# Rotating a 268 MB matrix by 90 degrees: borrowing the output buffers for the first two loads, dividing the last macro tile, and halving the last store

## The chip, the cores and the metric

The kernel runs on one core of one Trainium2 chip. Times are device microseconds of one execution. Groups of experiments ran on different chips, each beside its own runs of before, and only ratios are compared between groups. Ratios are computed as the mean time of one kernel's fast runs over the mean time of the other's fast runs of the same rounds on the same chip, so they are not quite the ratio of the medians that are quoted beside them. Kernels are counted "faster" or "slower" only beyond 2%.

## The reference

```python
def setup_inputs():
    return {"x": np.random.randn(8192, 8192).astype(np.float32), "k": 1}

def reference(x, k):
    return np.rot90(x, k)        # out[8191 - c, r] = x[r, c]
```

There is no arithmetic: 268 MB are read, 268 MB are written, and in between every element changes its place.

## The kernel before

The matrix is worked off in macro tiles of 1024 rows and 4096 columns. Each macro tile takes eight loads of 128 rows by 4096 columns (2 MB), which VectorE (DVE) copies into 64 small chunks, reversing the order of the columns within each block of 128. Then eight output groups follow: TensorE transposes 32 blocks of 128 by 128 into PSUM, ScalarE (ACT) evicts them in two copies, and one store writes 2 MB.

```python
R = 1024; RT = R // P; CH = 512; G = 4; PW = 2          # P = 128
def widths(first, last, M):
    return [M // 2] * 2
...
a_pool = ctx.enter_context(tc.tile_pool(name="a_pool", bufs=2))    # load buffers, 16 KB a partition
r_pool = ctx.enter_context(tc.tile_pool(name="r_pool", bufs=68))   # chunks, 2 KB a partition
o_pool = ctx.enter_context(tc.tile_pool(name="o_pool", bufs=2))    # output buffers, 16 KB a partition
psum_pool = ...                                                    # bufs=2, 8 KB a partition each
for r0 in range(0, N, R):
    c0 = 0
    for C in widths(r0 == 0, r0 + R == N, M):
        for t in range(RT):
            a = a_pool.tile([P, C], dt, tag="a")
            nc.sync.dma_start(out=a[:], in_=x[r0 + t*P : r0 + (t+1)*P, c0 : c0 + C])
            for j in range(C // CH):
                ... nc.vector.tensor_copy(...)     # each block's columns reversed, into a chunk
        for g0 in range(0, C // P, G):
            o = o_pool.tile([P, G, R], dt, tag="o")
            for h in range(0, G, PW):
                ... nc.tensor.transpose(...)       # 16 times into ps
                nc.scalar.copy(o[:, G - PW - h : G - h, :], ps[:])
            ...
            nc.scalar.dma_start(out=dst, in_=o[:]) # dst: four runs of 4 KB a partition
        c0 += C
```

A function `whole_reads`, run over the finished program, matters later. A store reads its 16 KB a partition from a contiguous output buffer, but the program describes that as four pieces of 1024 elements; `whole_reads` rewrites the source as one piece of 4096. The loads read one run of 16 KB a partition from the start.

Of the kernel before, what the change touches and what calls it, by code (L numbers as in the profile page):

```python
# [2 lines left out]

# [5 lines left out]

P = 128  # L10




R = 1024
RT = R // P
CH = 512
G = 4
PW = 2


def whole_reads(nc):






    for fn in nc.m.functions:
        for block in fn.blocks:  # L30
            for n, ins in enumerate(block.instructions):
                if not isinstance(ins, mybir.InstDMACopy):
                    continue
                src = ins.ins[0]
                ap = [list(d) for d in src.ap]
                if len(ap) == 3 and ap[2][0] == 1 and ap[1][0] == ap[2][1]:
                    ap = [ap[0], [1, 1], [1, ap[1][1] * ap[2][1]]]
                    block.instructions[n] = copy.replace(
                        ins,
                        ins=[copy.replace(src, ap=ap)],  # L40
                        ant_dge_precooked=False,
                    )


def widths(first, last, M):

    return [M // 2] * 2


@with_exitstack  # L50
def kernel(
    ctx: ExitStack,
    tc: tile.TileContext,
    x: bass.AP,
    k: bass.AP,
    out: bass.AP,
):
    nc = tc.nc
    assert k == 1, f"only k=1 supported, got {k}"
    nc.at_finalize(whole_reads)  # L60

    N, M = x.shape
    dt = x.dtype

    consts = ctx.enter_context(tc.tile_pool(name="consts", bufs=1))
    ident = consts.tile([P, P], dt)
    make_identity(nc, ident)

    a_pool = ctx.enter_context(tc.tile_pool(name="a_pool", bufs=2))
    r_pool = ctx.enter_context(tc.tile_pool(name="r_pool", bufs=68))  # L70
    o_pool = ctx.enter_context(tc.tile_pool(name="o_pool", bufs=2))
    psum_pool = ctx.enter_context(
        tc.tile_pool(name="psum", bufs=2, space=bass.MemoryType.PSUM)
    )

    for r0 in range(0, N, R):
        c0 = 0
        for C in widths(r0 == 0, r0 + R == N, M):
            chunks = {}
            for t in range(RT):  # L80
                a = a_pool.tile([P, C], dt, tag="a")
                nc.sync.dma_start(  # L82
                    out=a[:], in_=x[r0 + t * P : r0 + (t + 1) * P, c0 : c0 + C]
                )


                for j in range(C // CH):
                    ar = r_pool.tile([P, CH // P, P], dt, tag="ar")
                    nc.vector.tensor_copy(  # L89
                        out=ar[:],  # L90
                        in_=a[:, j * CH : (j + 1) * CH].rearrange(
                            "r (b m) -> r b m", m=P
                        )[:, :, ::-1],
                    )
                    chunks[t, j] = ar

            for g0 in range(0, C // P, G):
                o = o_pool.tile([P, G, R], dt, tag="o")
                for h in range(0, G, PW):
                    ps = psum_pool.tile([P, PW, R], mybir.dt.float32)  # L100
                    for w in range(PW):
                        g = g0 + h + w
                        for t in range(RT):
                            nc.tensor.transpose(  # L104
                                ps[:, PW - 1 - w, t * P : (t + 1) * P],
                                chunks[t, g * P // CH][:, g % (CH // P), :],
                                ident,
                            )
                    nc.scalar.copy(o[:, G - PW - h : G - h, :], ps[:])  # L109

                top = M - c0 - (g0 + G) * P
                dst = out[top : top + G * P, r0 : r0 + R].rearrange(
                    "(g m) f -> m g f", g=G
                )
                nc.scalar.dma_start(out=dst, in_=o[:])  # L115
            c0 += C


# [1 line left out]
_INS = ['x', 'k']  # L120
_OUTS = [((8192, 8192), 'float32')]

_NUMBERS = {'k': 1}


# [26 lines left out]
```

## Time and profile before

The median was 1278.4 us in three runs (1276.62 to 1279.38). The profiled execution took 1282.29 us, so it is a little slower than those runs.

First the page of the profile of before: busy time of PE, the busy tenths of the DMA engines and the rate in 40 equal slices, the two DMA queues (packets, MB, share of the engines' time; q1 carries the loads, q10 the stores), and the DMA issues (size, median us from issue to landing).

```profile
span 1280.5 us, 10385 instructions
...
PE 720.3 (56%) x4096; PEld 686.7 (54%) x4096; DVE 355.2 (28%) x1024; ACT 467.0 (36%) x257; POOL 0.7 (0%) x6
...
DMA  9999999999999999999999999999999999999988
GB/s 346 364 421 425 426 426 424 429 429 428 429 430 427 430 425 431 425 431 427 426 428 429 430 422 426 428 428 426 429 429 424 425 426 426 428 426 427 427 352 357
...
q1 hardware_dynamic: 18432, 268.44, 49.9%
q10 hardware_dynamic: 18432, 268.44, 49.4%
...
a<-in_x_dram SPq DMA_DIRECT2D x128, 2048.0 KB, 16.6
out_dram<-o ACTq DMA_DIRECT2D x128, 2048.0 KB, 15.9
```

The DMA engines are busy 90% or more in all but the last two slices. They move 421 to 431 GB/s from the third slice to the 38th, less in the first two (346 and 364) and in the last two (352 and 357), and TensorE is busy 56%. The kernel is a DMA stream with a slow start and a slow end. Both queues sent 18432 packets for 128 transfers (the page counts 4096 packets under 512 B, 16 for each of the 256 transfers). Where this text says packet, it means this record of the profile.

The head, in the timeline of before (start, duration, engine, line, operation, count, idle time before it and its releaser):

```profile
8.18 2.77 DVE L89 COPY ar<-a 128x512 f32<-128x512 f32 x8 [8.18 <-DMA a<-in_x_dram]
...
13.05 2.77 DVE L89 COPY ar<-a 128x512 f32<-128x512 f32 x8 [2.09 <-DMA a<-in_x_dram]
...
19.81 2.78 DVE L89 COPY ar<-a 128x512 f32<-128x512 f32 x8 [3.99 <-DMA a<-in_x_dram]
...
25.66 2.77 DVE L89 COPY ar<-a 128x512 f32<-128x512 f32 x8 [3.07 <-DMA a<-in_x_dram]
...
50.54 2.77 DVE L89 COPY ar<-a 128x512 f32<-128x512 f32 x8 [2.65 <-DMA a<-in_x_dram]
...
57.06 0.66 ACTq L115 DMA_DIRECT2D out_dram<-o  x1
```

DVE starts on a load when it has landed: all its 871.5 us of waits end with a load (below). The first two loads were queued together and landed 4.87 us apart. Later ones come 5.4 to 6.9 us apart, because there are only two load buffers and each next load is issued after the 2.8 us of copies that free one. The eighth load landed at 50.5 us, and the first store was issued at 57.06.

The waits of before (engine, line, what it waited for: total us, times, longest):

```profile
DVE ar L89 <- DMA a<-in_x_dram: 871.5, 128, 9.3
ACT o L109 <- DMA out_dram<-o: 750.7, 125, 11.5
```

DVE waits for loads and ACT waits for stores all along: both sides wait for the DMA.

The tail, in stretches of before (from:to, length, busy us and number of instructions of PE, weight loads, DVE, ACT, POOL; granted clock, DMA share, GB/s):

```profile
600.00:680.00 80.00, 47.93 (x263) 45.80 (x261) 22.20 (x64) 29.10 (x16) 0.00 (x0) 0.72 1.01 428
...
1220.00:1240.00 20.00, 15.25 (x110) 14.25 (x108) 2.77 (x8) 11.02 (x6) 0.00 (x0) 0.82 0.81 340
1240.00:1260.00 20.00, 13.27 (x100) 12.48 (x101) 0.00 (x0) 13.24 (x8) 0.00 (x0) 0.91 0.87 369
1260.00:1281.00 21.00, 7.05 (x63) 6.50 (x61) 0.00 (x0) 8.57 (x5) 0.00 (x0) 0.77 0.80 338
```

The last load's copies and the last two evictions of before, in its timeline:

```profile
1223.92 2.77 DVE L89 COPY ar<-a 128x512 f32<-128x512 f32 x8 [7.02 <-DMA a<-in_x_dram]
...
1269.37 3.63 ACT L109 COPY o<-ps 128x2048 f32<-128x2048 f32 x2 [2.50 <-DMA out_dram<-o]
```

The middle runs at 428 GB/s. The last load's copies start at 1223.92 us, nine stores are issued after that, and while stores run alone the rate is 338 to 369 GB/s.

### The profile page before, as it was taken

What the parts mean: (1) busy time and instruction counts of PE and PEld (TensorE: products, weight loads), DVE (VectorE), ACT (ScalarE), POOL (GpSimd) and SP (SyncE); (2) the same over time, 40 slices, a digit from 0 to 9 for tenths busy, and PEclk for the clock granted to TensorE, in tenths of its full rate; (3) what the DMA queues carried; (4) which work ended last, traced back from release to release, by engine and by line L of the source; (5) the groups of instructions that cost most, each with busy time, mean ns of one, the idle gap of its engine ahead of it and who ended that gap; (6) DMA issues with size and microseconds to landing.
All of it is one profiled execution on the core that took longest, in us unless ns stands there. A gap on an engine that the chain in (4) does not pass through costs nothing.

```text
span 1280.5 us, 10385 instructions
## 1 busy us (share of the span) xinstructions
PE 720.3 (56%) x4096; PEld 686.7 (54%) x4096; DVE 355.2 (28%) x1024; ACT 467.0 (36%) x257; POOL 0.7 (0%) x6
## 2 busy tenths in 40 slices
PE   0445555655665456565655655656556655655574
PEld 0345555655555456555555654555555645555474
DVE  3432223222322232233223222322232223222300
ACT  0233334333333343343334333433343334333455
POOL 0000000000000000000000000000000000000000
PEclk9967867687777877768677677686776777787778
DMA  9999999999999999999999999999999999999988
GB/s 346 364 421 425 426 426 424 429 429 428 429 430 427 430 425 431 425 431 427 426 428 429 430 422 426 428 428 426 429 429 424 425 426 426 428 426 427 427 352 357
DMA packets 36913, 537.55 MB, mean 420 GB/s; under 512 B 4096, under 2 KB 4096, under 8 KB 4096
## 3 DMA queue, kind: packets, MB, share of 16 engines
q1 hardware_dynamic: 18432, 268.44, 49.9%
q10 hardware_dynamic: 18432, 268.44, 49.4%
q8 instruction: 32, 0.52, 0.2%
q14 instruction: 17, 0.14, 0.0%
HBM read 268.44 MB, written 268.44 MB: 419 GB/s over the span
## 4 chain that ended last, share of the span: by engine, by line
DMA 79%; ACT 18%; PE 1%; DVE 1%; issue 1%; ACTq 0%; SPq 0%
DMA out_dram<-o 76%; ACT o L109 18%; DMA a<-in_x_dram 3%; PE ps L104 1%; DVE ar L89 1%; ACTq L115 0%; ACTq L109 0%; SPq L82 0%
## 5 line engine op out<-in xcount | busy, mean ns | idle before, releaser
L104 PE MATMUL ps<-ident,ar 128*128 128x128 f32 x4096 | 720.3, 358 | 548.6 <-ACT o L109 502.3
L104 PEld LDWEIGHTS ps<-ident,ar 128*128 128x128 f32 x4096 | 686.7, 192 | 581.9 <-ACT o L109 532.6
L109 ACT COPY o<-ps 128x2048 f32<-128x2048 f32 x256 | 465.7, 1871 | 805.3 <-DMA out_dram<-o 750.7
L89 DVE COPY ar<-a 128x512 f32<-128x512 f32 x1024 | 355.2, 422 | 871.5 <-DMA a<-in_x_dram 871.5
L109 ACT ACT_TABLE_LOAD x1 | 1.3, 1283 | 0.7 <-PEq L133 0.7
masks.py:199 POOL TENSOR_SCALAR_AFFINE_SELECT ident<-ident 128x128 f32<-128x128 f32 x1 | 0.3, 293 | 0.1
masks.py:197 POOL MEMSET ident<- 128x128 f32 x1 | 0.2, 204 | 0.3 <-POOLq L133 0.3
L133 POOL MEMSET const-bfloat16-1.0<- 128x1 bf16 x1 | 0.1, 101 | 0.0
L133 POOL MEMSET const-uint8-127<- 128x1 uint8 x1 | 0.1, 101 | 0.0
L133 POOL MEMSET const-float32-0.0<- 128x1 f32 x1 | 0.1, 98 | 0.2 <-issue 0.2
L133 POOL MEMSET const-float32-1.0<- 128x1 f32 x1 | 0.1, 98 | 0.0
## 6 DMA issues: line engine op xcount, KB each, us to landing
a<-in_x_dram SPq DMA_DIRECT2D x128, 2048.0 KB, 16.6
out_dram<-o ACTq DMA_DIRECT2D x128, 2048.0 KB, 15.9
```

The source lines that it names most:

```text
L89: nc.vector.tensor_copy(out=ar[:], in_=a[:, j * CH : (j + 1) * CH].rearrange("r (b m) -> r b m", m=P)[:, :, ::-1],)
L104: nc.tensor.transpose(ps[:, PW - 1 - w, t * P : (t + 1) * P], chunks[t, g * P // CH][:, g % (CH // P), :], ident,)
L109: nc.scalar.copy(o[:, G - PW - h : G - h, :], ps[:])
L133: nc = _bacc.Bacc("TRN2", target_bir_lowering=False, num_devices=1)
```

## The change

Its intent: (1) the two output buffers are idle in the first 50 us, so the first two loads land there and four loads can be queued at once; (2) the last macro tile is divided into 2048, 1024 and 1024 columns, so that its first columns can be stored while its last ones are still being loaded; a load stays at 2 MB by taking two or four row tiles at once; (3) the very last store goes out in two halves. The core of the diff:

```diff
+W = 4096
-def widths(first, last, M):
-    return [M // 2] * 2
+def macro_tiles(N, M):
+    for r0 in range(0, N, R):
+        widths = [W] * (M // W)
+        ...
+        if r0 + R == N:
+            widths[-1:] = [2048, 1024, 1024]
+        ...
+        q = W // C
-                a = a_pool.tile([P, C], dt, tag="a")
-                nc.sync.dma_start(out=a[:], in_=x[r0 + t*P : r0 + (t+1)*P, c0 : c0 + C])
+            if loads < 2:
+                a = o_pool.tile([P, W], dt, tag="o")
+            else:
+                a = a_pool.tile([P, W], dt, tag="a")
+            loads += 1
+            a = a.rearrange("r (q c) -> r q c", q=q)
+            nc.sync.dma_start(
+                out=a,
+                in_=x[r0 + t0*P : r0 + (t0+q)*P, c0 : c0 + C].rearrange("(q r) c -> r q c", q=q))
 ...
+            S = PW if last and g0 + G == C // P else G     # the last store in two halves
+                if done % S == 0:
+                    ... nc.scalar.dma_start(out=dst, in_=o[:, G - done : G - done + S, :])
```

More of the change, by code (lines that the diff above doesn't have):

```diff
@@ L42, in whole_reads @@
                     )
-def widths(first, last, M):
-    return [M // 2] * 2
+def macro_tiles(N, M):
+    for r0 in range(0, N, R):
+        widths = [W] * (M // W)
+        if r0 == 0:
+            widths[:1] = [4096]
+        if r0 + R == N:
+            widths[-1:] = [2048, 1024, 1024]
+        c0 = 0
+        for C in widths:
+            yield r0, c0, C
+            c0 += C
 @with_exitstack
@@ L74 @@
     )
-    for r0 in range(0, N, R):
-        c0 = 0
-        for C in widths(r0 == 0, r0 + R == N, M):
-            chunks = {}
-            for t in range(RT):
-                a = a_pool.tile([P, C], dt, tag="a")
-                nc.sync.dma_start(
-                    out=a[:], in_=x[r0 + t * P : r0 + (t + 1) * P, c0 : c0 + C]
-                )
+    tiles = list(macro_tiles(N, M))
+    loads = 0
+    for r0, c0, C in tiles:
+        last = (r0, c0, C) == tiles[-1]
+        q = W // C
+        chunks = {}
+        for t0 in range(0, RT, q):
+            if loads < 2:
[6 more added lines that the diff above has]
+                out=a,
+                in_=x[r0 + t0 * P : r0 + (t0 + q) * P, c0 : c0 + C].rearrange(
+                    "(q r) c -> r q c", q=q
+                ),
+            )
+            for u in range(q):
                 for j in range(C // CH):
@@ L90 @@
                         out=ar[:],
-                        in_=a[:, j * CH : (j + 1) * CH].rearrange(
+                        in_=a[:, u, j * CH : (j + 1) * CH].rearrange(
                             "r (b m) -> r b m", m=P
@@ L94 @@
                     )
-                    chunks[t, j] = ar
-            for g0 in range(0, C // P, G):
-                o = o_pool.tile([P, G, R], dt, tag="o")
-                for h in range(0, G, PW):
-                    ps = psum_pool.tile([P, PW, R], mybir.dt.float32)
-                    for w in range(PW):
-                        g = g0 + h + w
-                        for t in range(RT):
-                            nc.tensor.transpose(
-                                ps[:, PW - 1 - w, t * P : (t + 1) * P],
-                                chunks[t, g * P // CH][:, g % (CH // P), :],
-                                ident,
-                            )
-                    nc.scalar.copy(o[:, G - PW - h : G - h, :], ps[:])
-                top = M - c0 - (g0 + G) * P
-                dst = out[top : top + G * P, r0 : r0 + R].rearrange(
-                    "(g m) f -> m g f", g=G
-                )
-                nc.scalar.dma_start(out=dst, in_=o[:])
-            c0 += C
+                    chunks[t0 + u, j] = ar
+        for g0 in range(0, C // P, G):
+            ot = o_pool.tile([P, W], dt, tag="o")
+            o = ot.rearrange("m (g f) -> m g f", g=G)
+            S = PW if last and g0 + G == C // P else G
+            for h in range(0, G, PW):
+                ps = psum_pool.tile([P, PW, R], mybir.dt.float32)
+                for w in range(PW):
+                    g = g0 + h + w
+                    for t in range(RT):
+                        nc.tensor.transpose(
+                            ps[:, PW - 1 - w, t * P : (t + 1) * P],
+                            chunks[t, g * P // CH][:, g % (CH // P), :],
+                            ident,
+                        )
+                nc.scalar.copy(o[:, G - PW - h : G - h, :], ps[:])
+                done = h + PW
+                if done % S == 0:
+                    top = M - c0 - (g0 + done) * P
+                    dst = out[top : top + S * P, r0 : r0 + R].rearrange(
+                        "(g m) f -> m g f", g=S
+                    )
+                    nc.scalar.dma_start(
+                        out=dst, in_=o[:, G - done : G - done + S, :]
+                    )
 _INS = ['x', 'k']
```

## The prediction

> **What bounds the kernel now.** By the slices of the page the 16 DMA engines are busy 9 tenths or more from the second slice to the 38th, at 421 to 431 GB/s mostly; PE is busy 56%. [...]428 GB/s in the stretch 600 to 680 us agrees. 537 MB at 428 GB/s would be 1254 us (estimate), so about 25 of 1278 us lie at the ends:
> - Head: the first eight loads have no store beside them (timeline: DVE starts on them at 8.18, 13.05, 19.81, 25.66, 32.54, 38.44, 45.12, 50.54 us). Loads 1 and 2, queued together, land 4.87 us apart; later ones average 6.25, because each next load is issued only after the eight DVE copies (2.8 us) of an earlier one.
> - Tail: the last load's copies start at 1223.92 us; nine stores are issued after that, at 338 to 369 GB/s, until 1280.5.
>
> **What the change does.**
> 1. Loads 1 and 2 land in the two output buffers, idle until the first eviction at 53.24 us. So four loads are queued at the start; loads 3 and 4 should land 4.87 us apart, load 4 at about 22.7 us in place of 25.66. From load 5 on two buffers rule again, so the gain stays at 3 us: load 8 at about 47.5, first store at about 54 us in place of 57.06. The DMA is the limit afterwards, so the 3 us reach the end.
> 2. The last macro tile is cut into 2048, 1024 and 1024 columns. It keeps eight 2 MB loads and eight stores' worth in the same order, behind the previous tile's eight stores; in the built programs each DVE copy waits for the same transpose as before. The DMA shares itself about evenly, so loads stay eight to nine ahead of stores, as the head set it. The smaller tiles are ready earlier, but stores never waited for that (waits: ACT waits 750.7 us for output stores, DVE 871.5 us for loads). I expect nothing: nine stores still remain. The eight loads with 8 KB and 4 KB runs resemble the stores' 4 KB runs, which land no slower; cost near zero.
> 3. The last store is split into two 1 MB halves. It was issued at 1273.03, after two ACT copies of 1.87 us. Now one half goes 1.9 us earlier, the other 0.6 us later (one more ACT issue of 0.55 us) with half the data: 2.4 us less transfer. Estimate: 1.7 us gained.
>
> **Predicted time:** 1278.4 - 3.0 - 1.7 = 1273.7 us, range 1269.5 to 1277.5. Faster by over 2%: 0.02; within 2%: 0.97; slower by over 2%: 0.01.
>
> **What would show it right.** DVE groups starting at about 8, 13, 18, 23 us, then pairs 12.6 us apart; first store at about 54 us; middle slices still 421 to 431 GB/s; eight or nine stores' worth issued after the last load's copies start; the last two issues 1 MB each.
>
> **What would make it wrong.** Four queued loads might share the engines instead of landing in turn, so DVE works them off late and gain 1 is lost. If the smaller tiles let stores overtake loads, the tail has fewer stores and gains several us more. If 4 KB runs read slower, the stretch 1150 to 1220 us drops below 420 GB/s and costs a few us. A phase shift in the middle could move 0.2%.

## The result, and the profile after

The first measurement gave a median of 1276.18 us (four runs, 1275.77 to 1276.56) against 1278.89 us for before (four runs, 1276.62 to 1279.43): ratio 0.9982, 95% interval 0.9965 to 0.9999. Repeated later with more rounds (run all_three) it was 0.9979, 0.9967 to 0.9991. The change gains 2.3 to 2.7 us, about half of the 4.7 us forecast; the first interval ends just short of no gain at all. The time lies within the predicted range, the gain does not match the forecast one.

The page after the change:

```profile
span 1274.2 us, 10388 instructions
...
GB/s 375 366 427 427 427 428 431 429 428 428 430 428 430 428 427 429 429 429 429 427 427 427 429 427 428 427 427 429 428 427 426 424 423 429 427 425 422 420 408 338
...
q1 hardware_dynamic: 20480, 268.44, 49.8%
q10 hardware_dynamic: 18576, 268.44, 49.8%
...
out_dram<-ot ACTq DMA_DIRECT2D x2, 1024.0 KB, 5.7
```

Two things differ. The slow tail is shorter: the last slice but one runs at 408 GB/s where it was 352 (the last runs at 338 where it was 357). And the loads sent 20480 packets, 2048 more, although they move the same bytes: a 2 MB load of two row tiles makes 256 packets of 8 KB and one of four row tiles 512 packets of 4 KB, so four and four of them add 512 and 1536. The stores' count rose by 144, for the one extra DMA.

The head after (timeline):

```profile
17.87 2.77 DVE L111 COPY ar<-a 128x512 f32<-128x512 f32 x8 [2.13 <-DMA a<-in_x_dram]
...
22.76 2.77 DVE L111 COPY ar<-a 128x512 f32<-128x512 f32 x8 [2.12 <-DMA a<-in_x_dram]
...
47.89 2.77 DVE L111 COPY ar<-a 128x512 f32<-128x512 f32 x8 [2.66 <-DMA a<-in_x_dram]
...
54.41 0.64 ACTq L141 DMA_DIRECT2D out_dram<-ot  x1
```

Loads 3 and 4 land 4.9 us apart, as intended; from load 5 on the spacing is 5.4 to 7.1 us again. The first store is issued at 54.41 us.

The tail after (timeline):

```profile
1195.63 3.64 ACT L133 COPY ot<-ps 128x2048 f32<-128x2048 f32 x2 [3.62 <-PE ps L128]
...
1205.72 0.55 ACTq L141 DMA_DIRECT2D out_dram<-ot  x1
1205.74 2.77 DVE L111 COPY ar<-a 128x512 f32<-128x512 f32 x8 [7.11 <-DMA a<-in_x_dram]
1206.37 3.63 ACT L133 COPY ot<-ps 128x2048 f32<-128x2048 f32 x2 [7.10 <-DMA a<-in_x_dram]
...
1246.81 2.77 DVE L111 COPY ar<-a 128x512 f32<-128x512 f32 x8 [11.96 <-DMA a<-in_x_dram]
...
1249.99 0.55 ACTq L141 DMA_DIRECT2D out_dram<-ot  x1
...
1255.58 0.55 ACTq L141 DMA_DIRECT2D out_dram<-ot  x1
...
1261.06 0.55 ACTq L141 DMA_DIRECT2D out_dram<-ot  x1
...
1265.43 2.32 ACTq L141 DMA_DIRECT2D out_dram<-ot  x2
```

This is not what the prediction said. The last load's copies start at 1246.81 us, and only the stores issued at 1249.99, 1255.58, 1261.06 and the two halves come after it: four stores' worth, where before had nine. Stores overtook loads. But at 1199 us, where the eviction of 3.64 us ends, ACT stands still until 1205.72 (7.1 us by the waits of the profile, which count in 0.6 us of the issue), and what it waits for is a load: the copies of that load start 0.02 us later, on DVE. ACT cannot issue the store it has ready. The built program, not the trace, says why: it gives its DMAs eight completion counters in turn, and before this store (number 119) ACT waits until its counter shows that the fifth load of the divided tile (number 125), which used it before and is late, has landed. The DMA engines were not idle meanwhile: from 1199 to 1206 us they moved 413 GB/s, and the rate fell to 342 only from 1210 to 1215 us.

To see where time is lost I use one measure for all profiles: the length of a stretch less the MB moved in it over 428.5 GB/s (about the rate of the full middle, which is 425 to 429 GB/s in the stretches of before from 80 to 1140 us). The three columns are the first 80 us, 80 to 1140 us, and 1140 us to the end. Each profile is one execution, and some are not typical: that of tiles_pool_loads was the slowest of its six runs, those of head_buffers and head_and_tail_buffers the slowest of five and of four, that of small_loads_undivided the fastest of four.

| profile | span, us | lost in head | lost in middle | lost in tail |
|---|---|---|---|---|
| before | 1280.5 | 11.4 | 3.3 | 11.3 |
| before_twin | 1279.3 | 11.7 | 1.5 | 11.6 |
| the change | 1274.2 | 8.9 | 1.3 | 9.4 |
| all_three (the change again) | 1274.9 | 9.4 | 1.7 | 9.4 |
| head_only | 1276.8 | 9.2 | 1.8 | 11.4 |
| tiles_only | 1277.9 | 11.2 | 1.7 | 10.5 |
| half_only | 1278.1 | 11.5 | 2.2 | 9.9 |
| tiles_small_stores | 1278.1 | 11.3 | 0.7 | 11.7 |
| small_loads_undivided | 1288.0 | 8.1 | 1.3 | 24.1 |
| tiles_pool_loads | 1277.6 | 11.6 | 0.5 | 11.0 |
| tail_buffers | 1276.0 | 10.1 | 3.8 | 7.7 |
| head_buffers | 1273.4 | 4.1 | 3.1 | 11.7 |
| head_and_tail_buffers | 1269.7 | 4.3 | 2.1 | 8.8 |

The middle moves by up to 3.3 us between profiles whose middle is the same program. The head with two load buffers moves as much: from 8.1 to 11.7 us in its eight profiles (mean 10.9), against 8.9 to 9.4 in the three with the changed head (mean 9.2). So the 6.3 us between the two first spans are not the gain: 2.0 us of it lies in that middle.

### The profile page after: what moved, and what is told of

Same layout as the page of the kernel before. It is cut to its first block, busy times and chain, and to the rows that moved or that the text cites. A ratio compares the mean times of both kernels' runs of the same rounds, so it can differ in the third digit from the quotient of the medians.

```text
span 1274.2 us, 10388 instructions
## 1 busy us (share of the span) xinstructions
PE 719.2 (56%) x4096; PEld 685.5 (54%) x4096; DVE 355.2 (28%) x1024; ACT 466.9 (37%) x257; POOL 0.7 (0%) x6
## 3 DMA queue, kind: packets, MB, share of 16 engines
q1 hardware_dynamic: 20480, 268.44, 49.8%
## 4 chain that ended last, share of the span: by engine, by line
DMA 84%; DVE 12%; issue 2%; ACT 1%; PE 0%; DVEq 0%; SPq 0%; ACTq 0%
DMA a<-in_x_dram 81%; DVE ar L111 12%; DMA out_dram<-ot 3%; ACT ot L133 1%; PE ps L128 0%; DVEq L111 0%; SPq L100 0%; ACTq L133 0%; ACTq L141 0%
## 5 line engine op out<-in xcount | busy, mean ns | idle before, releaser
L133 ACT COPY ot<-ps 128x2048 f32<-128x2048 f32 x256 | 465.6, 1870 | 789.3 <-DMA out_dram<-ot 733.5
L133 ACT ACT_TABLE_LOAD x1 | 1.3, 1283 | 10.9 <-DVE ar L111 10.9
```

## The experiments

Theory of the packets, formed after the result: what a queue gets of the engines depends on the size of its packets, so a load cut in smaller packets than a store's falls behind, and the division acts through that. Rival one, that short runs are slow to read from memory. Rival two, the prediction's: the division does nothing. All edits are shown against the changed kernel.

### 1. Each part alone

```diff
 head_only:   -widths[-1:] = [2048, 1024, 1024]   +widths[-1:] = [4096]
              -S = PW if last and ... else G      +S = G
 tiles_only:  -if loads < 2:                      +if loads < 0:
              -S = PW if last and ... else G      +S = G
 half_only:   -widths[-1:] = [2048, 1024, 1024]   +widths[-1:] = [4096]
              -if loads < 2:                      +if loads < 0:
 all_three:   the changed kernel
```

> Only the first two loads in the output buffers; last tile undivided, last store whole. Both theories expect the head gain alone: DVE groups start near 8.1, 13.0, 17.9, 22.8, 29.8, 35.4, 42.5, 47.9 us, first store issued near 54.4 us (57.1 in before), last load's copies about 1221 us with nine stores issued after them. Time 2.7 us below before (ratio 0.9979). If the head gain is lost in the middle, ratio 1.000.

> Only the last macro tile divided; first loads and last store as before. Packet theory (formed from the trace after the change: a store packet is 16 KB, a load packet 8 or 4 KB there[...], so loads fall behind and stores overtake): last load's copies start near 1247 to 1250 us, about four stores issued after it, and the tail's deficit shrinks, but a part is lost again to a store held up by a load; time 1 to 3 us below before. The theory of the prediction: nine stores after the last load, ratio 1.000.

> Only the last store split into two halves. Expected by the prediction: 1.7 us below before (ratio 0.9987), with two 1 MB issues about 2.4 us apart at the end. Rival: the store ahead of it and the fixed time to landing hide it, gain under 0.7 us.

> The changed kernel once more, with more rounds. If the parts add up, its gain is the sum of head_only, tiles_only and half_only; if tiles and half store draw on the same idle time of the tail, it is less. On the first measurement 2.3 us below before (ratio 0.9982); if that was only the spread of the runs of before, 4 to 6 us as the two profiled spans (1280.5 and 1274.2) have it.

Measured, with five rounds, on one chip; before had a median of 1280.05 us in 11 runs:

| run | median, us | ratio | 95% interval |
|---|---|---|---|
| head_only | 1278.04 | 0.9988 | 0.9976 to 0.9999 |
| tiles_only | 1279.72 | 0.9999 | 0.9986 to 1.0012 |
| half_only | 1280.44 | 1.0000 | 0.9985 to 1.0016 |
| all_three | 1276.90 | 0.9979 | 0.9967 to 0.9991 |

The head is worth 1.5 us by the clock (0.1 to 3.1), so the clock alone only just leaves room for 3. In profiles, the first store is issued at 53.38, 54.41 and 54.83 us in the three kernels with this head (mean 54.2) and between 53.44 and 57.39 us in the eight profiles with the old head (mean 56.2): a gain of 2.0 us. The head itself came as predicted (about 54 us); the prediction compared it with one profile, 57.06, which is at the late end. The fastest of the eight had its eighth load at 47.06 us with two load buffers alone: when each load lands differs from run to run, and four loads queued at the start set only the first four.

The half store is lost in the timing, but the interval (a loss of 2.0 us to a gain of 1.9) does not rule out the predicted 1.7. The profiles must decide. In its profile the end looks like this:

```profile
1264.92 0.55 ACTq L141 DMA_DIRECT2D out_dram<-ot  x1
1267.46 3.63 ACT L133 COPY ot<-ps 128x2048 f32<-128x2048 f32 x2 [2.56 <-DMA out_dram<-ot]
1269.35 2.31 ACTq L141 DMA_DIRECT2D out_dram<-ot  x2
```

From the start of the last two evictions to the end of the span it is 10.64 us here (1278.1 less 1267.46), 10.66 and 10.62 in the two profiles of the change, and 11.04 to 11.16 in seven profiles that end with a whole store after a wait for one of the two output buffers (before, where it is 1280.5 less 1269.37, its twin, head_only, tiles_only, tiles_small_stores, small_loads_undivided, head_buffers). The halves are worth 0.5 us, as the rival in the expectation had it (under 0.7). The prediction treated the two halves as if the engines were free. They are not: the store before was issued at 1264.92 us and took 7.3 us to land, so it was still under way when the first half was issued at 1269.35; the halves took 5.4 and 6.0 us from issue to landing. Half the bytes took only 1.3 to 1.9 us off the 7.3. (The "fixed time to landing" of the expectation: in before the first load took 7.4 us from issue to landing and the second landed 4.87 us after it, so about 2.5 us of a landing are not transfer; an estimate from these two.) This profile's tail loss, 9.9, is 1.4 to 1.7 lower than in the two profiles of before; 0.5 of that is the end, and for the rest, one profile can't tell it from the way the last load happened to fall between two stores.

The division alone gave nothing by the clock (my 1 to 3 us missed), but not because nothing happened. In the profile of tiles_only the last load's copies start late, and four stores follow them:

```profile
1248.97 2.77 DVE L111 COPY ar<-a 128x512 f32<-128x512 f32 x8 [12.45 <-DMA a<-in_x_dram]
```

As in the change, ACT waited on a load from 1201 us on, 7.4 us in all.

The ratios of the three parts add up to a gain of 1.7 us, all three together gave 2.7; each is uncertain by about 1.5, so nothing follows from the difference.

### 2. Packet size, turned round both ways

tiles_small_stores is tiles_only with the last 16 stores left out of `whole_reads`, so that a store makes packets of 4 KB too (1928 packets for 7.65 MB, 1185 to 1220 us):

```diff
                 if len(ap) == 3 and ap[2][0] == 1 and ap[1][0] == ap[2][1]:
+                    seen[0] += 1
+                    if 112 < seen[0]:
+                        continue
```

small_loads_undivided keeps the last tile whole (with the old head and a whole last store) and cuts only the description of its eight loads in four, at the source and, without effect on the addresses, at the destination (abridged):

```diff
-            widths[-1:] = [2048, 1024, 1024]
+            widths[-1:] = [4096]
+                    if ins.engine == mybir.EngineType.SP and loads > 120:
+                        cut = [ap[0], [1024, 4], [1, 1024]]   # was [ap[0], [1, 4096]]
```

> As tiles_only, but the last 16 stores are issued in 4 KB packets in place of 16 KB ones (same bytes, same 4 KB runs in the output). Packet theory: [...]stores no longer overtake; the last load's copies start near 1215 to 1225 us again (1248.97 in tiles_only), eight or nine stores come after it, and no store waits on a load near 1200 us. Rival, that short runs from memory are slow to read: loads lag as in tiles_only, the last load near 1249 us.

> Last macro tile undivided, as before, but its eight loads are cut into 4 KB packets. Packet theory: the loads fall behind although the tile is whole; the stores of the tile before run ahead and then stop until the last load, so the last load's copies start near 1205 to 1220 us, with eight stores after it and a stretch just before it in which loads run alone; time equal to before within 2 us. If the column division alone made the loads fall behind, nothing changes against before: nine stores after the last load at about 1223 us, loads still 16.6 us from issue to landing.

tiles_small_stores has its last load's copies where before had them:

```profile
1220.40 2.77 DVE L115 COPY ar<-a 128x512 f32<-128x512 f32 x8 [7.59 <-DMA a<-in_x_dram]
```

Nine stores come after it, and no store waits on a load; the ratio is 0.9990 (0.9976 to 1.0003). The loads have the same 8 and 4 KB runs as in tiles_only, yet they no longer lag. So slow short reads are not what made them lag, and the packets of the *other* queue matter besides their own. The shares of the two queues show it. The middle of before, 1000 to 1100 us, 16 KB against 16 KB (queue, packets, MB, share of the engines; q1 loads, q10 stores):

```profile
q1 hardware_dynamic: 1455, 21.22, 50.3%
q10 hardware_dynamic: 1463, 21.35, 50.1%
```

tiles_only, 1222 to 1246 us, loads of 4 KB packets against stores of 16 KB:

```profile
q10 hardware_dynamic: 478, 6.87, 67.8%
q1 hardware_dynamic: 770, 3.03, 32.0%
```

tiles_small_stores, 1185 to 1220 us, 4 KB against 4 KB:

```profile
q10 hardware_dynamic: 1928, 7.65, 53.3%
q1 hardware_dynamic: 1713, 6.75, 47.0%
```

With equal packets the queues shared about evenly (50.3% and 50.1%, 47.0% and 53.3%); with a quarter of the packet size the loads got 32.0%. This repeats: the 4 KB loads got 31.8% in the change (1207 to 1241 us; 28.0% when taken to 1246), 33.6% in tiles_only from 1208 to 1222 us, 34.6% in tiles_pool_loads (1205 to 1245) and 33.5% in small_loads_undivided (1146 to 1188), though stretches of 8 us range from 26 to 48% in the change between 1206 and 1234 us. Loads of 8 KB against stores of 16 KB got 42.3% (1145 to 1185 us, the change), and in tiles_small_stores, where for a while the loads had the larger packets (mostly 8 KB against mostly 4 KB, 1150 to 1180 us), the shares turned round: 56.3% for the loads and 44.2% for the stores.

How the engines choose between the queues is not shown. Equal numbers of packets would give the 4 KB loads 20% (estimate, 4 of 4 + 16 KB); here 770 load packets went beside 478 store packets, or, by the MB and without the short ones, about 740 beside 419, 1.8 to 1. The profile does not show which part of that is time in which the store queue was empty.

small_loads_undivided: the loads fall behind although the tile is whole, so the packets and not the columns do it. The rest of the expectation missed: the last load came at 1232.54 us, not by 1220, and the time was 10.1 us longer than before by the medians (1291.47 against 1281.37 us; ratio 1.0082, 1.0067 to 1.0098), not equal. Two lines tell why:

```profile
1232.54 2.77 DVE L123 COPY ar<-a 128x512 f32<-128x512 f32 x8 [3.06 <-DMA a<-in_x_dram]
...
1235.24 1.87 ACT L145 COPY ot<-ps 128x2048 f32<-128x2048 f32 x1 [26.14 <-PE ps L140]
```

The stores of the tile before ran ahead and ended; then nothing could be evicted until the last load, and ACT stood 26.1 us. Just before, a held store had cost ACT 11.4 us more (a wait on a load, until 1205.46). Loads then run alone, at 410 and 412 GB/s from 1221.4 to 1228.8 us and at 231 until 1232.5, and after them eight stores run alone, 311 GB/s from 1234 us to the end. Without the division there is nothing to store while loads lag. So the smaller packets are what makes overtaking happen (last load at 1232.54 us with the tile whole, 1223.92 in before), and the division is what keeps it from costing time (ratio 0.9999 with it, 1.0082 without).

### 3. Does the held store take the division's gain back?

tiles_pool_loads issues the last eight loads from the POOL queue, whose completion counters are not shared with the stores:

```diff
-            nc.sync.dma_start(
+            queue = nc.gpsimd if loads > 120 else nc.sync
+            queue.dma_start(
```

> As tiles_only, but the last eight loads are issued from the POOL queue, so that their completion counters are no longer shared with the stores. Theory: in tiles_only a store of the tile before last stood 7.4 us because its completion counter was still in use by load 125, and this cost up to 2 us of DMA time; here no wait of ACT on a load between 1195 and 1210 us, the DMA stretch 1200 to 1230 us at 420 GB/s or more, loss from 1140 us to the end near 8.5 us (10.5 in tiles_only), time about 2 us below tiles_only (ratio to before 0.998). Rival: the wait cost nothing, since the engines were busy with loads; loss and time as tiles_only. Not clean if the loads from POOL get another share of the engines.

The ratio was 0.9984 (0.9972 to 0.9996; median 1278.53 against 1279.71 us), close to the 0.998 expected. The wait of ACT on a load (7.4 us in tiles_only) is gone, as the shared counters would have it, and 1200 to 1230 us runs at 427 GB/s, against 406 in tiles_only: worth 1.5 us in that stretch (30 us times 21/428.5). The loads' and stores' shares from 1205 to 1245 us are 34.6% and 66.9%, near those of tiles_only (33.6% and 67.9%, then 32.0% and 67.8%, between 1208 and 1246 us), so the other queue hardly changed the share. But the tail's loss in this profile, the slowest of the six runs, is 11.0, not 8.5: that part of my expectation missed. Unhindered, the stores ran on until they had caught up with the loads:

```profile
1256.39 2.77 DVE L112 COPY ar<-a 128x512 f32<-128x512 f32 x8 [11.49 <-DMA a<-in_x_dram]
...
1261.10 1.87 ACT L134 COPY ot<-ps 128x2048 f32<-128x2048 f32 x1 [7.32 <-PE ps L129]
```

The last load now lands at 1256.39 us, ACT waits 7.3 us for its transposes, and two stores with nothing beside them end the program (242 GB/s from 1260 us on). My reading is that the held store was a cost, and also a brake: too little overtaking leaves many stores alone, too much leaves the chain load, copy, transpose, eviction, store bare at the end. It rests on one profile of each kind and was not tested. The intervals of this ratio and that of tiles_only overlap, so the two cannot be ranked, and whether the held store took back the division's gain is not shown.

### 4. The limits themselves: two output buffers in the tail, two load buffers in the head

If the tail is slow because two output buffers cannot keep the engines busy, and the head because two load buffers cannot, then buffers and not column widths are the remedy, and idle ones exist at both ends.

```diff
 tail_buffers (last tile undivided, old head, whole last store):
-            ot = o_pool.tile([P, W], dt, tag="o")
+            if last and g0 // G % 4 < 2:
+                ot = a_pool.tile([P, W], dt, tag="a")
+            else:
+                ot = o_pool.tile([P, W], dt, tag="o")
 head_buffers (last tile undivided, whole last store):
-            if loads < 2:
+            if loads < 8 and loads % 4 < 2:
 head_and_tail_buffers: both
```

> Last tile undivided; four of its eight stores go out of the two load buffers, which are idle by then. Theory that the tail is bound by two output buffers (each cycle = landing 7.3 us + eviction 3.65 us for two buffers, 5.6 us a store): with four buffers the nine stores after the last load follow at 4.9 to 5.1 us each, the last stretch runs at 415 to 428 GB/s in place of 369, time 4 to 6 us below before (ratio 0.996). Rival, that stores alone cannot go faster than about 370 GB/s: ratio 1.000.

> tail_buffers plus loads 1, 2, 5 and 6 in the output buffers, so that four buffers take the first eight loads in turn. Expected: DVE groups 4.9 us apart all the way, load 8 at about 42.3 us (50.5 in before, 47.9 in the change), first store issued near 49 us, and this gain reaches the end: 7 to 8 us for the head and 4 to 6 for the tail, time about 1267 us (ratio 0.990). Rival: the head gain is eaten by the middle, ratio as tail_buffers.

> Only the head of head_and_tail_buffers: the first eight loads take four buffers in turn, the tail as before. If head and tail gains add up, 7 us below before (ratio 0.9945), with the loss of the first 80 us near 4.3 us (11.4 in before).

| run | median, us | before, us | ratio | 95% interval |
|---|---|---|---|---|
| tail_buffers | 1277.29 | 1281.37 | 0.9969 | 0.9956 to 0.9982 |
| head_buffers | 1272.91 | 1279.71 | 0.9949 | 0.9937 to 0.9961 |
| head_and_tail_buffers | 1269.94 | 1281.37 | 0.9913 | 0.9900 to 0.9927 |

A stretch of the tail in which stores run alone, tail_buffers first, then before (columns as above):

```profile
1235.00:1265.00 30.00, 22.05 (x191) 20.39 (x189) 0.00 (x0) 23.17 (x13) 0.00 (x0) 0.97 1.01 425
```

```profile
1230.00:1260.00 30.00, 22.44 (x177) 20.90 (x176) 0.00 (x0) 19.96 (x12) 0.00 (x0) 0.93 0.87 368
```

Stores alone ran at 425 GB/s here: the 368 of before was the turn-round of two output buffers. The gain is 4.0 us, at the low edge of the 4 to 6 expected; the tail still loses 7.7 us, part of it at 1225 to 1235 us (300 GB/s), where only stores run and the second of them is issued at 1232.06.

The head of head_buffers (timeline):

```profile
27.65 2.77 DVE L111 COPY ar<-a 128x512 f32<-128x512 f32 x8 [2.12 <-DMA a<-in_x_dram]
...
49.77 0.64 ACTq L141 DMA_DIRECT2D out_dram<-ot  x1
```

Load 5 lands 4.89 us after load 4 (22.76), load 8 at 43.25 (load 7 alone came 5.8 us after the one before), and the first store is issued at 49.77 us. The loss of the first 80 us is 4.1 in place of 11.4, and 6.5 us of it arrive at the end (0.51% of 1280). Both together gain 11.1 us (0.87% of 1280), close to the 10.5 us of the two alone. All outputs were correct. By their intervals this version beats before and the changed kernel (0.9967 to 0.9991).

### 5. The kernel before against itself

> The kernel before, unchanged, timed against itself: ratio 1.000 within 0.15%. Its profile says how much two profiles of one kernel differ: the loss in the first 80 us and from 1140 us to the end should be within 0.5 us of the first profile (11.4 and 11.3), while the middle may differ by 2 us.

Ratio 0.9997 (0.9983 to 1.0011), as expected; head and tail losses repeat within 0.3 us, the middle differs by 1.8. Two profiles were too few for the head: over all eight with two load buffers it loses 8.1 to 11.7.

## Why the prediction was right or wrong

- **"537 MB at 428 GB/s ... about 25 of 1278 us lie at the ends": right.** Given more buffers, 11 us of them came back.
- **Step 1, "the gain stays at 3 us": right in mechanism, wrong in size.** Loads 3 and 4 landed 4.9 us apart and the pairs followed, but the gain is 2.0 us by the mean first store (54.2 against 56.2 us) and 1.5 us by the clock (0.1 to 3.1, which just includes 3). What failed is the baseline: the term was measured against a single profile whose first store, at 57.06 us, was among the latest of eight. "The 3 us reach the end" holds in kind: in head_buffers a head gain of 7.3 us arrived as 6.5.
- **Step 2, "The DMA shares itself about evenly ... nine stores still remain": wrong.** In these runs it shared evenly only with packets of equal size (loads 50.3% and 47.0%). Loads of 8 and 4 KB packets fell behind (42.3% and 32.0%), and four stores' worth remained. The sentence that the 4 KB runs "resemble the stores' 4 KB runs" failed in the same place: the stores' runs are 4 KB in the output, but their packets were 16 KB (144 a store, 16 of them short), and became 4 KB in tiles_small_stores when the source alone was described in shorter runs. The number, no gain, still came out in the timing (0.9999, 0.9986 to 1.0012), but by luck. Why overtaking brought nothing is only argued: the profile has a held store (about 1.5 us against tiles_pool_loads) and a drained pipeline at the end. "If the smaller tiles let stores overtake loads" was listed as a risk, with "several us more"; it happened, and the several us did not come.
- **Step 3, "1.7 us gained": the term most mis-sized.** It measured 0.5 us. The estimate took the transfer time off the last store but forgot that a full store was still in front of the first half (issued 4.4 us before it, 7.3 us to land). Here the split paid only for the part of the last transfer that nothing else covered.
- **The sum.** 3.0 + 0 + 1.7 was forecast; 2.0 from the profiles' heads, 0 from the clock for the division and 0.5 from the profiles' ends make 2.5, beside 2.3 to 2.7 us measured. The forecast change was about twice the real one. This is no proof of each term: in both profiles of the change the tail loses 9.4 us, about 2 us less than in those of before, more than the 0.5 of the halves, and that rest does not show in the timing of tiles_only.

What stays open: why two-buffer heads take anything from 53.44 to 57.39 us to the first store, why the middle's loss moves between 0.5 and 3.8 us in one and the same program text, and why fewer stores alone in the tail brought so little.

## What to carry to other kernels

When a DMA-bound kernel loses time only at its ends, look for buffers that are idle there before reshaping tiles: four buffers in place of two brought both the loads of the head (417 GB/s from 8 to 43 us) and the stores of the tail (425) to within a few per cent of the full rate of 428, and the two gains added up. When two queues compete, compare their packet sizes first: here, changing the shape of one queue's transfers changed the share of both (the loads' from about 50% to 32%). And compare a forecast of a few us with several profiles of before, not with one.
